# Two-layer hybrid backbone on one core: query tiles loaded one tile ahead, and the modulation biases in a row of their own

## The chip, the cores and the metric

The kernel runs on one core of one Trainium2 chip. The metric is the device time of one execution in microseconds. Before the change the median of three runs is 3571.68 us (3569.08 to 3574.14).

## The reference

Two layers, each a feed-forward half-step, a token mixing and a second feed-forward half-step, over 512 latent tokens and 256 context tokens of width 1024. Nine rows per layer (shift, scale and gate of the three parts) come from the conditioning vector by a product with a bias:

```python
def ada_mod(cond, w, b):
    m = jax.nn.silu(cond) @ w + b
    return m.reshape(cond.shape[:-1] + (N_MOD, D_MODEL))
```

The token mixing has three groups of heads from one input projection: a Fourier group, a banded attention in which each query tile of 128 tokens sees its neighbours and all context keys, and a bidirectional recurrence:

```python
def window_attention(q, k, v, kc, vc, sink):
...
    s_w = jnp.einsum('bnqhgd,bnkhd->bnhgqk', qb, kw)
    s_c = jnp.einsum('bnqhgd,bchd->bnhgqc', qb, kc.astype(f32))
...
def wkv_step(state, inp):
    r, w, k, v, a, b = inp
    sa = jnp.einsum('zbhij,zbhj->zbhi', state, a)
    state = state * w[..., None, :] + sa[..., None] * b[..., None, :] + v[..., None] * k[..., None, :]
    y = jnp.einsum('zbhij,zbhj->zbhi', state, r)
    return state, y
```

Their outputs go through one output projection. Everything is in float32.

## The kernel before, in words

**The mixer.** In each layer the recurrence is computed in six groups of 256 tokens (context forward and backward, then latent tokens in both directions). The work of a group is `stage_a` (products of the group's keys and queries), `inverses` (the inverse of a triangle for every chunk of 64 tokens), `stage_c` (each chunk's map of the state) and `chain` (the states, one after the other), and for three of them a `readout`. The mixer of layer 0 runs its recurrence from about 895 to 1281 us, and its tail (the rest of the output projection) to 1419 us; that of layer 1 has its recurrence from about 2732 to 3118 us.

**An inverse.** Two tiles of operands (W) are read from DRAM (`opd`), 24 pairs of small products give the triangles, ACT copies these from PSUM into LAB (L961), DVE cuts out the 32x32 blocks, a DMA stores them in DRAM (`d0`, L975), and another reads them back in another layout (L976), with a leading dimension of 2 whose stride is zero. Then DVE runs 31 dependent steps of two instructions (L987, L989). A store and a load in the other layout follow (L992, L993), and then the products of `stage_c`.

**What is put between.** The attention (60 units of scores or outputs in layer 0), the modulations of the following parts (18 halves in layer 0, 8 in layer 1) and the output projection of the attention heads (12 parts, `out_part`, L1532) don't depend on the recurrence. `pump` hands them out as the recurrence's work goes on. Beyond that a scheduler in the compiler, which simulates a timeline, sets the order of the instructions on every engine, so a small edit can move work over long stretches. All DMAs here are issued by SP on one hardware queue, in the order of the program on SP.

**Queries.** For each token tile `queries(b)` issues a DMA of 128x6x128 elements into the tile q (one buffer, L1062), whose source has a leading dimension of 2 with a stride of zero; ACT casts it to the high parts qs (L1064), POOL makes the low ones.

**Modulations.** A half of a modulation is three steps: `part(0)` and `part(1)` each load 1 MB of weights (wmod, L251) and multiply by quarters of the array (L256) into PSUM; `total` copies the 128x512 sums to the tile macc (L262), loads the bias into row 2 of it (L263), and sums rows 0, 1, 32, 33 and so on and the bias by a product with the constant `sel4` (L266 or L271).

Of the kernel before, what the change touches and what calls it, by code (L numbers as in the profile page):

```python
# [8 lines left out]
F32 = mybir.dt.float32  # L9
# [23 lines left out]
# tiles of the feed-forward columns in the chunks after the first; buffers of gated products: raw (then low), high  # L33
# [5 lines left out]
class Halves:  # L39
    """Products of weights and tokens by Strassen's scheme (Winograd's form): the halves are of the  # L40
    inner dimension, of the tokens, and gates with values; 7 products of quarters instead of 8."""

    def __init__(self, net, n0, n):
        self.net, self.nc, self.w = net, net.nc, n // 2
        hi, lo = net.hT["h"], net.hT["o"]
        m = self.w
        q = lambda x, t, k: x[:, 4 * k:4 * k + 4, n0 + t * m:n0 + t * m + m]
        self.a = {f"a{t + 1}{k + 1}": (q(hi, t, k), q(lo, t, k)) for t in range(2) for k in range(2)}
        # the quarter a21 isn't needed by itself
        self.a["s3"] = self.a["a21"]  # L50

    def sums(self, anchor):
        """The second half of the work comes behind the anchor."""
        nc, a, net, m = self.nc, self.a, self.net, self.w
# [30 lines left out]
    def weights(self, wi, c0):  # L85
        """The quarters of a tile of gates and one of values, and their sums."""
# [13 lines left out]
    def unit(self, ws, sg, pool):  # L100
        """silu(gates) * values."""
# [4 lines left out]
        for i, nm in enumerate(("a11", "a12", "s2", "s1", "s3", "s4", "a22")):  # L106
            ps = net.pst.tile([128, 512], F32, name="pq", tag="a")
            a, w = self.a[nm], ws[i]
            j = 0
# [34 lines left out]
# buffers of the ring of weights that stay through the mixers' projections, and more: raw, split  # L144
# [3 lines left out]
class Net:  # L148
# [78 lines left out]
    def behind(self, inst, anchor=None):  # L227
        """The engine of both issues inst after the anchor."""
# [10 lines left out]
    def mod_steps(self, l, m, wp, pf):  # L239
        """Steps for the modulation m of layer l: the sums by quarters of the array, then their sums with the bias."""  # L240
# [3 lines left out]
        for h in range(2):  # L244
# [3 lines left out]
            def part(q, cs=cs, st=st):  # L248
# [3 lines left out]
                if q == 0:  # L252
                    st["ps"] = pf([128, 512])
                for g in range(4):
# [4 lines left out]
            def total(h=h, cs=cs, st=st):  # L259
                self.mark('modt')  # L260
                acc = wp.tile([128, 512], F32, name="macc", bufs=1)
                nc.scalar.copy(acc, st["ps"])  # L262
                self.dma(acc[2:3], self.a["mod_b"][l:l + 1, cs])  # L263
# [12 lines left out]
    def mod(self, l, ms, stg, rows):  # L276
        """The modulations ms (at most two) of layer l."""
# [34 lines left out]
    def norm_cols(self, l, n, m_shift, m_scale):  # L312
        """Columns of g*(1+scale) and of shift, by stream."""
# [8 lines left out]
    def gate_row(self, l, n, m, s, half):  # L322
        """The row half*m*g, on all partitions."""
# [11 lines left out]
    # The arena's tiles hold rows in turn (4), loaded rows (2), halves of transposes (2) and gate rows (2);  # L335
    # in the feed-forward halves the sums of quarters of the normed tokens
# [18 lines left out]
    # In the passage from one part to the next the engines keep to the order of the program  # L355
# [10 lines left out]
    def squares(self, x, junk):  # L366
        """The root of the mean of the squares."""
# [18 lines left out]
    def prenorm(self, t, x, cols, xn, junk):  # L386
        """Normalises the token tile t; every second one is transposed with the one before it. Two steps."""
# [11 lines left out]
    def flush(self, rest=True):  # L399
        """Emits the transposes that were put off, behind products that needn't wait for them."""  # L400
# [8 lines left out]
    def some(self, n=1):  # L409
        """What follows the transposes, by quarters."""  # L410
        for _ in range(min(n, len(self.bits))):
            self.bits.pop(0)()
# [37 lines left out]
    def residual(self, t, o, grow, xn, po):  # L450
        """x + norm(o)*grow for the token tile t, with o's halves as they come. Three steps."""
# [3 lines left out]
        for i in range(2):  # L455
            cs = slice(i * 512, i * 512 + 512)
            # of the halves' mean squares
# [11 lines left out]
    def passage(self, toks, outs, post):  # L469
        """The last products of the tokens, by halves (outs), and what follows them, a token behind."""  # L470
# [27 lines left out]
    def load_w(self, srcs, shape):  # L498
        """Loads weights (pieces by columns, or by rows of two dimensions)."""
# [11 lines left out]
    def turning(self, j, name, shape, dt):  # L511
        """The next tile of the ring, raw (0) or split (1)."""
# [9 lines left out]
    def cut(self, x, e=None):  # L522
        """Splits x, of at most 512 columns in all, exactly: (high, low), each of float32r."""
# [9 lines left out]
    def split_w(self, srcs, shape, e=(None, None)):  # L533
        """Weights, split exactly, by halves of their first free dimension."""
# [4 lines left out]
    def prod(self, ps, w, s, c0, n):  # L539
        """Sums in ps the products of the weights w with n tokens of stream s, from c0."""  # L540
# [13 lines left out]
    def ffn(self, l, wi, wo, toks, post, last, mods=(), early=None):  # L554
        """last: loads that follow the last chunk's products with the tokens."""
# [10 lines left out]
        # the last 64 columns come first: gates and values in one tile  # L566
# [12 lines left out]
        def split_g(sg, w):  # L579
            gh = fp.tile([128, NT], F32R, name="gh", bufs=GB)  # L580
            if w == 64:
                # the low parts below the high ones
# [10 lines left out]
        def gated(sg, cs, w, pg, pu):  # L593
            """silu(gates) * values; of a tile with both, on its upper half."""
# [9 lines left out]
        def first(ch):  # L604
            """The first chunk, by pairs of token tiles, as they become ready."""
# [81 lines left out]
    def early_keys(self, l, raw):  # L687
        """The context's keys of the recurrence, while the latent tokens are on their way."""
# [10 lines left out]
    def mixer(self, l, need_ctx):  # L699
# [5 lines left out]
        with self.pool("mixo", bufs=1) as mo, ExitStack() as outer:  # L705
# [8 lines left out]
            # partial output projections: of the Fourier heads, and of the attention heads as well  # L714
            self.part = [[self.dp.tile([128, D], F32, name=f"part{l}_{j}_{i}") for i in range(6)] for j in range(2)]
            # decays over the chunks
            pcs = mo.tile([128, 2, 3, 12], F32, name="pcs")
            self.rw = dict(pcs=pcs)
            # in DRAM: head sums times values; values in token-major; queries; by direction the recurrence's
            # unit keys by the decay so far, rates and keys by its inverse, receptances by the decay  # L720
# [6 lines left out]
            # keys' high parts, on both halves, by head; low parts  # L727
# [5 lines left out]
            with self.pool("inp", side="right") as rp, ExitStack() as inner:  # L733
# [5 lines left out]
                def load(c0):  # L739
                    """Columns c0 (a list of pieces) of the input projection's weights, split."""  # L740
                    return self.split_w([win[:, :, c:c + w] for c, w in (c0 if isinstance(c0, list) else [(c0, 128)])], [128, 8, 128])

                def proj(c0, ctxs=True, pcx=None):
                    """Columns c0 of the input projection: (latent, context) in PSUM."""
# [9 lines left out]
                # the recurrence's inputs; the context's first, while the latent tokens are on their way  # L754
                self.mark('inp')
                # rows 96 to 101: the heads' rows scaled by k_k
# [65 lines left out]
                # row 64: ones, and the decays' bias  # L822
# [23 lines left out]
                def operands(z):  # L846
                    """The recurrence's operands of direction z."""
# [11 lines left out]
                    for p in range(3):  # L859
# [11 lines left out]
                        # av: twice the in-context rate, less one  # L871
# [26 lines left out]
                for p in range(3):  # L898
                    r = rs[p]
                    v = conv(6 + p, kns[p], True)  # L900
                    # values, token-major
# [9 lines left out]
                    # the heads' sums of products of keys and receptances, times the values  # L911
# [10 lines left out]
    def diagonals(self, pool):  # L922
        """The recurrence's operands of two heads, on the blocks of a diagonal; KI: keys beside it, identities on it."""
# [13 lines left out]
    def triangles(self, pool):  # L937
        """Buffers of the inverses of the recurrence's triangles."""
# [4 lines left out]
    def inverses(self, gi, z, t0, psum, mm):  # L943
        """Of a group of 256 tokens from t0, direction z, the products of rates and unit keys, and the inverses of
        their 32x32 blocks on the diagonal."""
# [18 lines left out]
        # the blocks on the diagonal, of every unit a row of blocks; their inverses  # L964
# [811 lines left out]
```

## Time and profile before

| | |
|---|---|
| median of three runs | 3571.68 us (3569.08 to 3574.14) |
| span of the profiled execution | 3573.4 us |
| PE busy | 3262.0 us, 91% |
| DVE busy | 2352.3 us, 66% |
| ACT busy | 1378.0 us, 39% |
| POOL busy | 809.4 us, 23% |

The profiled execution has no other time than its span, which lies inside the runs' range and 1.7 us above their median. Busy shares are averages over the whole span; what an edit is worth depends on what the engines wait for in the stretch that it touches, and both edits touch only the two mixers.

### The profile page before, as it was taken

The numbers are of one execution on the slowest core, as the hardware profiler recorded it, in microseconds if no ns is written. First come the engines' busy times: TensorE is split into PE (matmuls) and PEld (weight loads), VectorE is DVE, ScalarE is ACT, GpSimd is POOL, SyncE is SP. The second block draws the span as 40 slices with busy tenths as digits, with TensorE's granted clock in tenths as the row PEclk, the third lists the DMA queues.
The fourth block names the chain that finished last, engine by engine and source line by source line (L and its number), as shares of the span: only waits on it lengthen the run. The fifth ranks groups of instructions, "written<-read, shape, count | busy, mean of one in ns | idle before, by whom it ended". The sixth has DMA issues, their size and how long they took to land. (4 is left out here: it accounts for less than half of the span.)

```text
span 3573.4 us, 51830 instructions
## 1 busy us (share of the span) xinstructions
PE 3262.0 (91%) x19801; PEld 2729.5 (76%) x19801; DVE 2352.3 (66%) x4374; ACT 1378.0 (39%) x2818; POOL 809.4 (23%) x609
## 2 busy tenths in 40 slices
PE   7999998998778897999998999998995898979998
PEld 5689997776556655899997899997774676758997
DVE  4577777456466656677777767777464666467897
ACT  3333335342334334433335433335342433344444
POOL 0222222023101013322222322222041000024333
PEclk9999999999889988999999999999997878779999
DMA  5432224245667556222224222224355563253333
GB/s 179 148 119 71 71 69 138 87 141 134 153 172 177 160 187 214 60 69 68 71 71 140 61 71 65 71 71 138 97 166 119 157 157 71 68 182 89 101 107 101
DMA packets 540346, 410.13 MB, mean 115 GB/s; under 512 B 210405, under 2 KB 462188, under 8 KB 540098
## 3 DMA queue, kind: packets, MB, share of 16 engines
q1 hardware_dynamic: 540098, 406.82, 39.4%
q8 instruction: 156, 2.56, 0.3%
q14 instruction: 92, 0.75, 0.1%
HBM read 345.60 MB, written 61.16 MB: 114 GB/s over the span
## 5 line engine op out<-in xcount | busy, mean ns | idle before, releaser
L666 PE MATMUL po<-wq,gh 128*128 128x512 f32 (+1 forms) x1936 | 692.4, 408 | 43.6 <-ACT po L458 23.8
L529 ACT CAST wq<-raw 128x512 fp32r<-128x512 f32 (+1 forms) x626 | 383.7, 619 | 619.0 <-PE pq L112 438.8
L112 PE MATMUL pq<-hh,wq 128*128 128x384 f32 (+1 forms) x2432 | 612.8, 324 | 5.1 <-DVE st L132 2.1
L530 DVE TENSOR_TENSOR wq<-raw,wq 128x512 fp32r<-128x512 f32 x616 | 510.5, 838 | 102.3 <-ACT wq L529 97.0
L112 PE MATMUL pq<-arena,wq 128*128 128x384 f32 (+1 forms) x2736 | 491.5, 324 | 1.7 <-ACT st L116 1.1
L666 PEld LDWEIGHTS po<-wq,gh 128*128 128x128 f32 (+1 forms) x1936 | 368.6, 191 | 152.6 <-ACT po L458 31.0
L112 PEld LDWEIGHTS pq<-arena,wq 128*128 128x128 f32 x2736 | 451.3, 189 | 24.1 <-issue 4.3
L112 PEld LDWEIGHTS pq<-hh,wq 128*128 128x128 f32 x2432 | 431.6, 188 | 19.5 <-issue 5.7
L112 PE MATMUL pq<-ho,wq 128*128 128x384 f32 (+1 forms) x1216 | 394.1, 324 | 0.0
L666 PE MATMUL po<-wq,go 128*128 128x512 f32 x924 | 371.0, 402 | 2.6 <-DVE go L590 2.6
L529 ACT CAST wq<-t 128x512 fp32r<-128x512 f32 x228 | 140.7, 621 | 340.6 <-PE pq L112 303.2
L93 POOL TENSOR_TENSOR t<-raw 128x512 f32<-128x512 f32 x76 | 103.6, 1363 | 735.8 <-DVE wq L530 358.6
L672 DVE TENSOR_TENSOR accl<-accl,po 128x512 f32<-128x512 f32 x288 | 196.8, 684 | 100.8 <-PE po L666 99.0
L112 PEld LDWEIGHTS pq<-ho,wq 128*128 128x128 f32 x1216 | 229.3, 189 | 7.1 <-issue 0.9
L544 PE MATMUL pil<-hh,wq 128*128 128x512 f32 (+1 forms) x704 | 217.0, 387 | 7.9 <-DVE hh L432 5.6
L666 PEld LDWEIGHTS po<-wq,go 128*128 128x128 f32 x924 | 177.1, 192 | 32.5 <-DVE go L590 5.7
L530 DVE TENSOR_TENSOR wq<-t,wq 128x512 fp32r<-128x512 f32 x228 | 176.4, 779 | 28.3 <-ACT wq L529 23.5
L544 PE MATMUL pc<-hh,wq 128*128 128x256 f32 x976 | 179.1, 284 | 6.4 <-DVE hh L432 5.1
L97 POOL TENSOR_TENSOR t<-raw,t 128x512 f32<-128x512 f32 x76 | 117.1, 1540 | 283.2 <-DVE wq L530 283.1
L987 DVE TENSOR_TENSOR W<-W 96x126 f32<-96x126 f32 (+22 forms) x372 | 101.8, 275 | 113.1 <-DMA W<-d 106.1
L544 PEld LDWEIGHTS pil<-hh,wq 128*128 128x128 f32 x704 | 133.1, 200 | 39.1 <-DVE hh L432 6.0
L544 PEld LDWEIGHTS pc<-hh,wq 128*128 128x128 f32 x976 | 152.6, 191 | 7.6 <-DVE hh L432 5.9
(386 smaller groups left out, 5670.6 us busy)
## 6 DMA issues: line engine op xcount, KB each, us to landing
raw<-in_ffn_wi_dram SPq DMA_DIRECT2D x168, 512.0 KB
wmod<-in_mod_w_dram SPq DMA_DIRECT2D x52, 1024.0 KB
raw<-in_ffn_wo_dram SPq DMA_DIRECT2D x84, 512.0 KB
raw<-in_mix_w_in_dram SPq DMA_DIRECT2D x38, 512.0 KB
raw<-in_mod_w_dram SPq DMA_DIRECT2D x24, 512.0 KB
x_l<-arena SPq DMA_DIRECT2D x20, 512.0 KB
arena<-x_l SPq DMA_DIRECT2D x20, 512.0 KB
W<-opd SPq DMA_DIRECT2D x24, 384.0 KB
```

The source lines that it names most:

```text
L93: e.tensor_sub(t1, b12, b11)
L97: e.tensor_sub(t4, b21, t2)
L112: net.last_mm = nc.tensor.matmul(ps[:, :m], lhsT=w[x][:, k], rhs=a[y][:, k], start=(j == 0), stop=(j == 11))
L529: nc.scalar.copy(q[:, 0], x)
L530: (e or nc.vector).tensor_sub(q[:, 1], x, r32(q[:, 0]))
L544: inst = self.nc.tensor.matmul(ps[:, :n], lhsT=w[kt // 4][wp][:, kt % 4], rhs=self.hT[s, hp][:, kt, c0:c0 + n], start=(j == 0), stop=(j == ...
L666: mm = nc.tensor.matmul(ps, lhsT=x[r, t0:t0 + 128], rhs=w[hf][y][r], start=(j == 0), stop=(j == len(todo) - 1))
L672: self.pin(nc.vector.tensor_add(acc[t][:, cs], acc[t][:, cs], ps))
L987: e.tensor_mul(tv, LB[:, i, ro][:, :, None].to_broadcast([96, n, w]), XB[:, i, co][:, None, :].to_broadcast([96, n, w]))
```

## The change

The load of a tile of queries becomes a function of its own, `fetch(b)`. It is called once when the attention's steps are set up, and then in `queries(b)`, behind the cast and the subtractions, for the next tile. The bias of a half of a modulation is loaded in `part(0)`, into row 98 of a tile that stays (`self.macc`, allocated once per mixer, its rows 96 to 127 set to zero by POOL); `total` copies rows 0 to 95 and 96 to 97 apart, so that row 98 isn't overwritten, and `sel4` has its one in row 98 instead of row 2.

```diff
@@ def mod_steps
             def part(q, cs=cs, st=st):
...
                 if q == 0:
                     st["ps"] = pf([128, 512])
+                    self.dma(self.macc[98:99], self.a["mod_b"][l:l + 1, cs])
...
             def total(h=h, cs=cs, st=st):
                 self.mark('modt')
-                acc = wp.tile([128, 512], F32, name="macc", bufs=1)
-                nc.scalar.copy(acc, st["ps"])
-                self.dma(acc[2:3], self.a["mod_b"][l:l + 1, cs])
+                acc = self.macc
+                for r in (slice(0, 96), slice(96, 98)):
+                    nc.scalar.copy(acc[r], st["ps"][r])
@@ def attention
-        def queries(b):
-            t = ap.tile([128, 6, 128], F32, name="q", bufs=1)
+        def fetch(b):
+            t = held["t"] = ap.tile([128, 6, 128], F32, name="q", bufs=1)
             src = self.qd[:, 0, 0, b * 128:b * 128 + 128]
             self.dma(t, bass.AP(tensor=src.tensor, offset=src.offset, ap=[[0, 2], [6 * NT, 64], [NT, 6], [1, 128]]))
+        def queries(b):
+            t = held["t"]
             q = ap.tile([128, 6, 128], F32R, name="qs", bufs=QB)
             nc.scalar.copy(q, t)
...
             held["q"] = q
+            i = order.index(b) + 1
+            if i < len(order):
+                fetch(order[i])
...
-        units = [(b, i) for b in ((4, 5, 0, 1, 2, 3) if need_ctx else range(4)) for i in range(3)]
+        order = (4, 5, 0, 1, 2, 3) if need_ctx else (0, 1, 2, 3)
+        fetch(order[0])
+        units = [(b, i) for b in order for i in range(3)]
@@ before the mixer's pump
             mp = stack.enter_context(self.pool("mods", side="right"))
+            self.macc = mp.tile([128, 512], F32, name="macc", bufs=1)
+            nc.gpsimd.memset(self.macc[96:128], 0.0)
@@ consts
-    c["sel4"] = (((p % 32)[:, None] == np.arange(2)) | (p == 2)[:, None]).astype(f)
+    c["sel4"] = (((p % 32)[:, None] == np.arange(2)) | (p == 98)[:, None]).astype(f)
```

The scheduler's order follows. On SP, at the start of the recurrence of layer 0, where inverse 1 loads its operands (W), stage A of the same group its own (AtB, BtB, KI, HB), and the attention its first queries (q), the order before is:

```order
L918 DMA bvd_5302<-kn_5558 128x768
L1321 DMA Z<-vtd_5303 64x12x64 x2
L954 DMA W_7429<-opd_5305 128x3x256 x2
L1062 DMA q<-qd_5304 128x6x128
L1285 DMA AtB<-opd_5305 64x12x64 x2
L1285 DMA BtB<-opd_5305 64x12x64 x2
```

And with the change:

```order
L251 DMA wmod<-in_mod_w_dram 128x4x512 x2
L254 DMA macc<-in_mod_b_dram 1x512
L911 DMA vtd_5303<-vk 384x1x64 x4
L919 DMA bvd_5302<-kn_5558 128x768
L1331 DMA Z<-vtd_5303 64x12x64 x2
L1063 DMA q<-qd_5304 128x6x128
L955 DMA W_7429<-opd_5305 128x3x256 x2
L1295 DMA AtB<-opd_5305 64x12x64 x2
```

The first load of queries has moved from behind the two loads of W to ahead of them, and the first modulation's weights and bias ahead of both.

On SP, at inverse 2 of layer 0 (counted from 0), the store of its blocks in DRAM (d_0_2), the read of them (W from d_0_2) and what stands between them, before:

```order
L975 DMA d_0_2_8363<-W_6655 128x12x32
L1140 DMA mixd_5288<-ob 128x3x128
L1321 DMA Z<-vtd_5303 64x12x64 x2
L263 DMA macc<-in_mod_b_dram 1x512
L976 DMA W_6655<-d_0_2_8363 96x1x1024
L954 DMA W_7429<-opd_5305 128x3x256
L992 DMA d_0_1_7788<-W_7429 1536x1x16 x2
```

And with the change:

```order
L976 DMA d_0_2_8367<-W_6655 128x12x32
L254 DMA macc<-in_mod_b_dram 1x512
L1331 DMA Z<-vtd_5303 64x12x64 x2
L251 DMA wmod<-in_mod_w_dram 128x4x512
L955 DMA W_7429<-opd_5305 128x3x256
L993 DMA d_0_1_7793<-W_7429 1536x1x16 x2
L251 DMA wmod<-in_mod_w_dram 128x4x512
L1063 DMA q<-qd_5304 128x6x128
L977 DMA W_6655<-d_0_2_8367 96x1x1024
```

The read of the blocks, on which the 31 steps on DVE wait, now stands behind the results of inverse 1, two loads of weights and a load of queries.

On PE, in layer 0, where the first part of the attention heads' output projection stands (products of omh and om with ow into pf). Before, the first of its 9 products is row 2998 on PE, among attention products (at) and the last readout's neighbours (pb):

```order
L1261 MATMUL pb<-HB 128x256 x4
L1083 MATMUL at<-k_5308,qs 128x256
L1084 MATMUL at<-kl,qs 128x256
L1083 MATMUL at<-k_5308,qs 128x256
L1084 MATMUL at<-kl,qs 128x256
L1532 MATMUL pf<-ow_9823,omh 128x512
L1261 MATMUL pb<-HB 128x256 x2
L1532 MATMUL pf<-ow_9823,om 128x512
```

With the change it is row 2929, among the products of the recurrence (stage A into pa, stage C into pb, the chain into pz):

```order
L1271 MATMUL pb<-HB 128x128 x4
L1271 MATMUL pz<-Z,HB 64x64
L1545 MATMUL pf<-ow_9825,omh 128x512
L1545 MATMUL pf<-ow_9825,om 128x512
L1545 MATMUL pf<-ow_9826,omh 128x512
L1545 MATMUL pf<-ow_9832,omh 128x512
L1545 MATMUL pf<-ow_9832,om 128x512
L1545 MATMUL pf<-ow_9833,omh 128x512
L1545 MATMUL pf<-ow_9839,omh 128x512
L1545 MATMUL pf<-ow_9839,om 128x512
L1545 MATMUL pf<-ow_9840,omh 128x512
L1271 MATMUL pa<-HB,BtB 128x128 x4
```

Counted over the whole of layer 0's mixer: ahead of the last products of the recurrence's last chain, PE had 53 of the 60 attention units, 17 of the 18 halves of modulations and none of the 12 parts of the output projection; with the change it has 60, 18 and 5. From the first step of inverse 1 to the end of inverse 5 DVE had 580 instructions, 310 of them steps; with the change it has 642. In layer 1 three of the parts come early, as before. The recurrence's own order on PE is the same, and so are the numbers of DMAs; ACT has 26 copies of 2x512 more, POOL two memsets.

## Rows read from the trace of the kernel before

**Rows 1.** The page's head, and busy time, share of span, instructions of PE.

```profile
span 3573.4 us, 51830 instructions
...
PE 3262.0 (91%) x19801; PEld 2729.5 (76%) x19801; DVE 2352.3 (66%) x4374; ACT 1378.0 (39%) x2818; POOL 809.4 (23%) x609
```

**Rows 2.** Windows of layer 0: length, busy time (instructions) by engine, clock, DMA share.

```profile
961.00:1211.00 250.00, 201.98 (x1963) 149.28 (x1965) 171.98 (x579) 104.28 (x276) 24.35 (x22) 0.88 0.65 159
1211.00:1281.00 70.00, 69.50 (x656) 49.24 (x656) 35.91 (x97) 28.63 (x76) 3.36 (x6) 0.95 0.67 196
1281.00:1419.00 138.00, 107.03 (x422) 71.42 (x415) 80.39 (x143) 58.13 (x132) 40.47 (x35) 0.85 0.67 211
```

**Rows 3.** PE's waits, 880 to 1330: us in total, times, longest.

```profile
PE pz L1261 <- DVE MG L1352: 22.5, 2, 13.7
PE pa L1261 <- ACT LAB L961: 8.5, 1, 8.5
```

**Rows 4.** PE's waits in layer 1, 2715 to 3170.

```profile
PE pf L266 <- DMA macc<-in_mod_b_dram: 7.9, 1, 7.9
```

**Rows 5.** DVE's waits, 895 to 1290.

```profile
DVE W L987 <- DMA W<-d: 57.6, 5, 17.2
```

**Rows 6.** Timeline of SP, PE and ACT around the first queries of layer 0.

```profile
905.06 1.27 SPq L954 DMA_DIRECT2D W<-opd  x2
906.38 0.56 SPq L1062 DMA_DIRECT2D q<-qd  x1
...
910.80 0.39 PE L1261 MATMUL pa<-W 64*64 64x64 f32 x6
...
921.19 0.83 ACT L1064 CAST qs<-q 128x768 fp32r<-128x768 f32 x1 [10.52 <-DMA q<-qd]
921.93 0.64 ACT L961 COPY LAB<-pa 128x256 f32<-128x256 f32 x2
...
922.35 0.48 PE L1261 MATMUL pa<-W 64*64 64x64 f32 x4 [8.52 <-ACT LAB L961]
```

**Rows 7.** DMA view, 906 to 922, in 40 slices of 0.4 us: busy tenths, GB/s.

```profile
DMA  9999999994111131111111111111389599211795
GB/s 208 255 160 166 189 312 353 358 343 137 40 40 42 41 82 42 41 42 41 41 42 41 41 42 41 42 41 41 99 204 221 110 209 182 33 24 28 180 242 102
```

**Rows 8.** Timeline of SP and DVE at inverse 2 of layer 0.

```profile
992.77 0.65 SPq L976 DMA_DIRECT2D W<-d  x1
...
1003.20 0.19 DVE L987 TENSOR_TENSOR W<-W 96x31 f32<-96x31 f32 x1 [7.81 <-DMA W<-d]
```

**Rows 9.** PE by line, 895 to 1419: count, busy us, mean ns; idle before.

```profile
L256 PE MATMUL pf<-wmod,cTz 128*32 128x512 f32 x288 | 41.7, 675 | 6.7 <-ACT mcol L272 6.7
...
L1532 PE MATMUL pf<-ow,omh 128*128 128x512 f32 x72 | 29.8, 470 | 10.1 <-ACT omh L1504 6.9 <-ACT ow L1522 1.6 <-DVE oo L1534 1.5
L1135 PE MATMUL at<-ptb,vt 128*64 128x128 f32 x264 | 25.7, 293 | 1.5 <-DVE ptb L1130 1.2 <-ACT ptb L1130 0.3
...
L1084 PE MATMUL at<-kl,qs 64*128 64x256 f32 (+1 forms) x60 | 24.4, 406 | 0.0
L1083 PE MATMUL at<-k,qs 128*128 128x256 f32 (+1 forms) x60 | 24.2, 404 | 0.7 <-ACT ob L1138 0.4 <-ACT pr L1106 0.3
...
L1129 PE MATMUL at<-ident,pr 128*128 128x128 f32 x132 | 22.7, 295 | 4.0 <-ACT pr L1115 2.2 <-ACT pr L1106 1.4 <-DVE ptb L1130 0.3
...
L1532 PE MATMUL pf<-ow,om 128*128 128x512 f32 x36 | 16.9, 471 | 0.9 <-POOL om L1506 0.9
```

**Rows 10.** DVE by line, 961 to 1211.

```profile
L987 DVE TENSOR_TENSOR W<-W 96x126 f32<-96x126 f32 (+21 forms) x154 | 43.7, 285 | 49.0 <-DMA W<-d 46.1
L989 DVE TENSOR_TENSOR W<-W 96x56 f32<-96x56 f32 (+22 forms) x155 | 43.1, 279 | 3.0
```

**Rows 11.** Instructions of the tile macc: durations in ns, first and last start.

```profile
L267 ACT COPY macc<-pf x10: 559/575/577, 947.9 to 2937.7; 2x512 f32<-2x512 f32 x10
```

## The prediction

> **What bounds the kernel now.** I began with the page's head: PE is busy 3262.0 of 3573.4 us [rows 1], so nearly all that is to be had lies in the 311 us in which PE idles, and an edit on SP, ACT or DVE counts only as far as it shortens or lengthens such an idle stretch. Both edits touch the two mixers alone, so I read these in windows. In layer 0 there are three stretches with different limits [rows 2]. From 961 to 1211 us PE idles 48 of 250 us while DVE is busy for 172: here the recurrence's dependences set the pace. From 1211 to 1281 PE is busy 69.5 of 70. From 1281 to 1419, the tail, it is busy 107 of 138.
>
> Next I read who waits for whom. PE's own list of waits names DVE products of the recurrence (MG, 22.5 us) and the copy LAB on ACT (8.5) [rows 3]. Behind the first stands what DVE waits for: the first of the 31 steps of an inverse waits for the read of its blocks, five times, 57.6 us in all and up to 17.2 [rows 5]. The 310 steps in the window cost DVE 43.7 + 43.1 = 86.8 us [rows 10], in which the remaining DVE instructions find room. So in this stretch the bound is a serial chain, from the store and read of an inverse's blocks over its steps to the products. In layer 1 the list has the row for LAB again, word for word as in layer 0, and one wait for a bias (7.9) [rows 4]; in layer 0 the waits for a bias are too short to be named.
>
> **Part 1: the queries.** The edit is to load queries a tile ahead. I looked at every load of queries: eight of the ten are issued a tile ahead already, and in their timeline no cast waits for its DMA; so there the edit gives nothing. Two casts wait, the first of each layer. In layer 0 the load is issued at 906.38 and the cast runs at 921.19; the LAB copies of inverse 1 stand behind the cast on ACT (921.93), and PE, which has done the first products of that inverse from 910.80, waits 8.52 us until 922.35 [rows 6]. What that load takes is seen in the DMA view: behind 910 us, when only it is in flight, the 16 engines are busy to about one or two tenths and move some 41 GB/s, for 7 us [rows 7]. A load whose source begins with a dimension of 2 is thus carried by few engines.
>
> The page "DMA: Bandwidth & Descriptors" of the Trainium skill, section "Why a DMA increments its semaphore by 16 and not by 1", states that the number of engines is the largest up to 16 that divides both patterns' slowest dimension, here 2; its "Rules for kernel authors" name the leading broadcast of c copies as confined to c engines. The trace agrees (a share of one to two tenths against 2/16 = 0.125). By that rule the change only moves the slow load, and loads issued behind it wait for it on those engines.
>
> With the change this load stands ahead of the two loads of W on SP, which move back by about 0.6 us, the time of its issue. It starts two issues earlier, 906.38 - 905.06 = 1.3 us, and lands perhaps that much earlier. But a part of each W that goes to the same engines comes behind it, so the products that PE starts at 910.80 begin as late as the cast does now, about 920; they and the first LAB copies have then the 1 to 3 us of the path behind them that now lie hidden ahead of the cast. If on the other hand it landed before W does, the whole 8.5 us would be saved. I take 0 for each layer, from -8.5 to +3.
>
> **Part 2: the biases.** The load moves from behind the copy of the sums to behind the first weights' load. Where PE waits for it now, 7.9 us in layer 1 [rows 4], the bias is due a whole pair of weight loads earlier, and I take -5 (0 to -7.9), since the half's closing products then go to a PE that idles elsewhere beside the recurrence too. In layer 0 there is nothing of note to save. The price is a second copy on ACT for each half: 26 of 2x512 elements at 0.575 us [rows 11], as long as a copy of 128 rows, 15 us of an engine that is 39% busy. I count it at 0: the copy stands behind a pair of weight loads, on which the next half waits in any case. Without that cover it would be 0.6 us for each half, 10 us in layer 0. The tile has one buffer as before: the bias of the next half waits until the closing products have read the last one. POOL's two memsets are ahead of the first sums and cost nothing.
>
> **Part 3: what the scheduler moved.** This is the largest part. Seven attention units, one half of a modulation and five of the 12 output parts stand ahead of the recurrence's end which stood behind it. From the PE groups: 24.4 + 24.2 + 25.7 + 22.7 = 97 us for 60 units, 1.6 each; 41.7 us for 18 halves, 2.3 each; 29.8 + 16.9 = 46.7 for 12 parts, 3.9 each [rows 9]. That is 7 x 1.6 + 2.3 + 5 x 3.9 = 33 us of PE.
>
> The tail gains: if it were PE's work alone, all 33; it is busy 107 of 138, and its waits are for ACT's squares and splits, which partly stay. I take two thirds, -22 (0 to -33).
>
> The recurrence pays. First, the read of inverse 2's blocks is now behind one load of queries and two of weights on SP. Now it is issued at 992.77 and DVE begins its steps at 1003.20, after a stall of 7.8 us [rows 8]. The read is of the same kind as the queries' (384 KB moved, leading dimension of 2), so both share the same few engines and it should land later by about what the one takes, 7 us in the DMA view [rows 7] up to the 10.5 that the cast stalls for the other [rows 6]: I take +9.5. Second, DVE has 642 instead of 580 instructions between the first step of inverse 1 and the end of inverse 5. Those that are not steps cost (171.98 - 86.8) / (579 - 309) = 0.32 us each [rows 2, 10], and up to 0.4 for the larger ones, so 62 more are 20 to 25 us. They fall partly into the 57.6 us in which DVE waits for the blocks [rows 5], where they cost nothing, and partly between steps, where each lengthens the chain. I take a fifth, +4.5, for most of the attention's units come in front of an inverse's first step, not among the steps. In sum +14; the bounds are 0 (the new work fills the waits, and the read is waited for no longer than now) and 10.5 + 25 = +36. In layer 1 the chain of inverses gets some 6.7 us more of DVE work and one read behind one more store: +3 (0 to 6.7).
>
> **Sum.** 0 + 0 - 5 - 22 + 14 + 3 = -10 against the profiled span of 3573.4, which lies 1.7 us above the median: 3571.7 - 10 = 3562. All bounds at their best would be -17 - 8 - 33 = -58, at their worst 6 + 36 + 7 = +49.
>
> **The rivals.** The measurement can tell about 0.2% from no change, 7 us.
>
> A. The forecast: the tail gains more than the recurrence pays, near 3562, by itself from 3553 to 3569. Chance 0.40.
>
> B. PE's idle time takes in all that was moved: 48 us idle from 961 to 1211 [rows 2] are more than 33. Then the recurrence pays nothing, the tail gains 33: 3571.7 - 33 - 5 + 3 = 3537. Against it speaks that PE idles there because it waits for the same DVE chain that the moved work feeds. Chance 0.12.
>
> C. The change does not do what it says: the scheduler had put eight of ten loads ahead already, the two first stay late, and what the tail gains the recurrence pays (22 each): -5 + 3, about 3570. For it speaks that PE is the bound over the mixers as a whole, and its work is the same. Chance 0.24.
>
> D. Slower. The read of inverse 2's blocks behind a load of queries on the same few engines delays the chain by 10, and the 20 to 25 us of DVE work stand among the steps rather than in the waits, which have then become no shorter: +34 for the recurrence, +6.7 in layer 1, -22 and -5: 3571.7 + 14 = 3585. It decides where the recurrence is lengthened by more than some 24 us, what the tail and the bias give back less the 3 of layer 1. For it speaks the stall of up to 17.2 us that such a read causes already [rows 5]. Chance 0.24. The rule that the Trainium skill states in "DMA: Bandwidth & Descriptors" leads there too, since it puts both reads on the same two engines.
>
> **How the numbers follow.** The predicted time is A's. Faster by over 0.2%: A but for the part near no change (0.36) and B (0.12), 0.48. Slower: D, and the part of C above (0.04), 0.28. Within 0.2%: the rest, 0.24. The range reaches from B's 3537, a little over it, to beyond D's 3585 by 5, for D's terms have bounds above what I took: 3536 to 3590.
>
> **What would show it.** Right: in the profile after, the stretch from the end of the recurrence in layer 0 to the feed-forward half is 138 - 22 = 116 us or so, the stretch before it longer by 14, and PE's wait for the bias in layer 1 is gone. The wait of PE for LAB at inverse 1 is there still, near 8 us, or has become a wait for W. DVE's longest wait for an inverse's blocks is the one of inverse 2, near 17. Wrong: if the first cast no longer waits and PE's LAB wait is gone (then up to 17 us better); if DVE's waits for blocks shrink while the recurrence is no longer (B); if they stay and the recurrence is longer by 25 or more (D); or if the clock that PE is granted in the mixers (0.88 and 0.85 in two of the windows [rows 2]) changes with the new order, of which I have no estimate.

## The result, and the profile after

The changed kernel takes 3597.0 us (median of 4 runs, 3595.5 to 3599.4), the kernel before 3572.9 beside it: a ratio of 1.0060, 95% interval 1.0039 to 1.0081. It is 24 us slower where 10 us faster was forecast, and 7 us beyond the range.

The profiled execution has a span of 3597.5 us. Set beside the same instructions before, work is 13 us late when layer 0 leaves its mixer, some 16 us where layer 1's begins, and 24 us behind it. The page's head answers to [rows 1]: PE is busy 19 us longer with the same 19801 products, and idle for 316 us in place of 311.

```profile
span 3597.5 us, 51852 instructions
...
PE 3281.1 (91%) x19801; PEld 2737.7 (76%) x19801; DVE 2354.5 (65%) x4374; ACT 1391.3 (39%) x2842; POOL 809.6 (23%) x611
```

The fixed windows of [rows 2] no longer hold the same work, so I cut layer 0's mixer at the end of the recurrence (DVE's last Z copy). The columns are the stretch, its length, busy time and count of PE, PEld, DVE, ACT and POOL, PE's granted clock, DMA share and GB/s. The kernel before, recurrence and tail:

```profile
870.00:1275.00 405.00, 333.60 (x3079) 244.64 (x3077) 240.78 (x763) 159.65 (x410) 34.90 (x35) 0.89 0.66 167
1275.00:1480.00 205.00, 170.90 (x898) 128.05 (x898) 130.32 (x217) 90.61 (x194) 50.88 (x40) 0.88 0.48 152
```

And the changed kernel:

```profile
871.00:1323.00 452.00, 382.00 (x3227) 276.30 (x3225) 256.96 (x812) 186.02 (x472) 40.49 (x41) 0.87 0.63 162
1323.00:1493.00 170.00, 145.02 (x749) 109.70 (x750) 115.22 (x168) 72.85 (x148) 45.66 (x35) 0.85 0.47 151
```

The recurrence is 47 us longer, the tail 35 us shorter. In the recurrence PE idles 405 - 333.6 = 71 us before and 452 - 382 = 70 after: **on balance none of the moved work went into idle time**. PE is busy 48 us longer there, with 148 more products, and 26 less in the tail. What is left, 22 us, is the same work taking longer, and the clock column says why in part: the share is a mean of 1 and 0.5, so 0.89 of 405 us means 2 x 0.11 x 405 = 89 us at 1.2 GHz in place of 2.4, and 0.87 of 452 us 118. These 22 us can't be laid to the change: two executions of the order of before differ by as much (first_not_ahead, below, has PE busy for 526.9 us over the same products, the kernel before for 504.5).

PE's waits in layer 0 after, to be held against [rows 3]: the chain's waits have become shorter (for MG 11.7 us in place of 22.5, for Z 2.4 in place of 8.1), and waits for loads stand in their place.

```profile
PE pf L272 <- DMA macc<-in_mod_b_dram: 14.2, 1, 14.2
PE pf L257 <- DMA wmod<-in_mod_w_dram: 12.6, 2, 6.4
PE pb L1271 <- DVE MG L1362: 7.9, 1, 7.9
PE pb L1271 <- ACT HB L1353: 7.7, 1, 7.7
```

DVE's waits for the blocks of the inverses, to be held against [rows 5], have also become shorter; beside them stand 17.7 us for which no releaser is named:

```profile
DVE W L988 <- DMA W<-d: 30.2, 3, 15.2
```

Around inverse 2 ([rows 8]) SP's timeline shows the load of queries ahead of the read of the blocks, and DVE's first step, 26 us later than before:

```profile
1005.51 0.55 SPq L1063 DMA_DIRECT2D q<-qd  x1
1006.11 10.13 SPq L977 DMA_DIRECT2D W<-d  x1
...
1022.16 3.14 SPq L254 DMA_DIRECT2D macc<-in_mod_b_dram  x1
...
1029.46 0.19 DVE L988 TENSOR_TENSOR W<-W 96x31 f32<-96x31 f32 x1 [15.17 <-DMA W<-d]
```

The second row's 10.13 us is SP held in one issue while the loads ahead are under way; the bias on which PE waits (14.2) stands behind both. In layer 1 PE's two longest waits at the first queries before were

```profile
PE pa L1261 <- DMA W<-opd: 18.6, 1, 18.6
PE pa L1261 <- ACT LAB L961: 8.5, 1, 8.5
```

One row takes their place after, and no wait for a bias is left there:

```profile
PE at L1091 <- POOL qs L1072: 26.9, 1, 26.9
```

### The profile page after: what moved, and what is told of

It is laid out like the page before. It is cut to its first block, busy times and chain, and to the rows that moved or that the text cites. A ratio compares the mean times of both kernels' runs of the same rounds, so it can differ in the third digit from the quotient of the medians.

```text
span 3597.5 us, 51852 instructions
## 1 busy us (share of the span) xinstructions
PE 3281.1 (91%) x19801; PEld 2737.7 (76%) x19801; DVE 2354.5 (65%) x4374; ACT 1391.3 (39%) x2842; POOL 809.6 (23%) x611
## 5 line engine op out<-in xcount | busy, mean ns | idle before, releaser
L531 DVE TENSOR_TENSOR wq<-raw,wq 128x512 fp32r<-128x512 f32 x616 | 501.3, 823 | 104.1 <-ACT wq L530 98.7
```

The lines of the kernel that those rows point to most:

```text
L531: (e or nc.vector).tensor_sub(q[:, 1], x, r32(q[:, 0]))
```

## The experiments

The ratio is to the kernel before in the same job, with its 95% interval.

| run | median us | ratio | interval |
|---|---|---|---|
| the change | 3597.0 | 1.0060 | 1.0039 to 1.0081 |
| q_alone | 3598.9 | 1.0072 | 1.0047 to 1.0098 |
| b_alone | 3596.7 | 1.0060 | 1.0040 to 1.0080 |
| q_split | 3541.7 | 0.9898 | 0.9878 to 0.9918 |
| d_split | 3517.4 | 0.9835 | 0.9815 to 0.9855 |
| before_q_split | 3520.5 | 0.9831 | 0.9813 to 0.9848 |
| before_d_split | 3492.6 | 0.9749 | 0.9717 to 0.9781 |
| both_split | 3468.2 | 0.9684 | 0.9664 to 0.9704 |
| before_both_split | 3459.9 | 0.9661 | 0.9644 to 0.9678 |
| before_pace_122 | 3580.3 | 1.0012 | 0.9992 to 1.0032 |
| before_pace_128 | 3567.1 | 0.9984 | 0.9971 to 0.9998 |
| after_pace_120 | 3577.7 | 1.0011 | 0.9994 to 1.0027 |
| after_pace_130 | 3580.8 | 1.0027 | 1.0011 to 1.0043 |
| later_fetch | 3586.6 | 1.0032 | 1.0016 to 1.0048 |
| first_not_ahead | 3577.8 | 1.0006 | 0.9992 to 1.0019 |
| bias_by_act | 3591.4 | 1.0059 | 1.0037 to 1.0080 |
| two_bias_rows | 3594.0 | 1.0066 | 1.0044 to 1.0087 |
| layer0_only | 3583.1 | 1.0028 | 1.0015 to 1.0041 |
| layer1_only | 3572.9 | 0.9994 | 0.9975 to 1.0014 |

**One edit at a time.** q_alone has the hunks of `fetch` and `queries` alone, b_alone those of `mod_steps`, `macc` and `sel4`.

> The edit of the queries alone; the biases as before. The loads of queries that stand ahead of inverse 2's read of its blocks in the changed kernel stand behind it here, and the modulations keep their places. Theory 1 (the slow loads of queries and blocks, which few DMA engines carry, stand one behind the other in the changed kernel, and the bias behind both): only the first load of each layer is ahead of W now, PE's wait for LAB becomes a wait for W, within 0.2% of the kernel before, 3567 to 3580 us. Theory 2 (work that is moved ahead of the recurrence's end lengthens it, and the lower clock makes the same products longer, whatever the DMAs do): nothing is moved here, so the time is that of before too. Theory 3 (the first load of queries ahead of W is the cost): 3585 to 3597.

> The edit of the biases alone; the queries as before. The modulations are pulled ahead as in the changed kernel, but no load of queries stands between inverse 2's store of its blocks and their read. Theory 1: inverse 2's read lands some 12 us behind its issue, no bias is waited for over 8 us in layer 0, and the time is nearer to the kernel before than to the changed one, 3570 to 3584. Theory 2: the order alone costs, the time is that of the changed kernel, 3590 to 3600, with the recurrence of layer 0 some 50 us longer and the tail shorter.

Each alone costs what both cost together, so the costs don't add, and theories 1 and 2, which both let q_alone be, fail on it: it has no load of queries ahead of inverse 2's read, and hardly any work moved. Its one profile has the recurrence at 436 us all the same, with 28 more products than before, PE idle for 62 us and a granted clock of 0.82; this profile is of one of its slower executions (3612 us). Theory 3 came nearest to its time. b_alone's time came out as theory 2 says; its recurrence is 440 us long, some 35 longer than before where theory 2 said 50.

**The slow loads.** The leading dimension of 2 is taken away, in the changed kernel and in the kernel before:

```diff
-self.dma(t, bass.AP(tensor=src.tensor, offset=src.offset, ap=[[0, 2], [6 * NT, 64], [NT, 6], [1, 128]]))
+for v in range(2):
+    self.dma(t[64 * v:64 * v + 64], bass.AP(tensor=src.tensor, offset=src.offset, ap=[[6 * NT, 64], [NT, 6], [1, 128]]))
```

```diff
-self.dma(LB, bass.AP(tensor=d0.tensor, offset=d0.offset, ap=[[0, 2], [1024, 48], [1, 1024]]))
+for v in range(2):
+    self.dma(LB[48 * v:48 * v + 48], bass.AP(tensor=d0.tensor, offset=d0.offset, ap=[[1024, 48], [1, 1024]]))
```

> The changed kernel with each load of queries as two DMAs of 64 partitions by 6x128 elements, without the leading dimension of 2, in nearly the same order on SP. Theory 1: a load of queries lands 3 to 5 us behind its issue in place of 13, inverse 2's read no longer lands 30 us behind its store, PE's wait for a bias of 14 us in layer 0 is gone, and PE's wait of 27 us in layer 1 is shorter by 8 or more; the time falls by 12 us or more, 3570 to 3585. Theory 2: the DMAs were covered; 3592 to 3600.

> The changed kernel with each read of an inverse's blocks as two DMAs of 48 partitions by 1024 elements, without the leading dimension of 2; the queries as in the changed kernel. Theory 1: each read lands 3 to 6 us behind its issue in place of 10 to 16, so DVE's waits for blocks fall by 6 us for each of 10 inverses, and the time falls by 15 to 40 us, 3557 to 3582. Theory 2: the chain gains, but the moved work takes it back: 3585 to 3597.

> The kernel before with each load of queries as two DMAs of 64 partitions, for comparison with the changed kernel with the same split (3542 us). Theory 1 (the change costs because slow loads on few engines stand one behind the other): with the split the change costs nothing, so this one takes 3535 to 3550. Theory 2 (the moved work and the clock): the change costs some 20 us here as well, so this one takes 3515 to 3528.

> The kernel before with each read of an inverse's blocks as two DMAs of 48 partitions, for comparison with the changed kernel with the same split (3517 us). Theory 1: within 8 us of it, 3510 to 3526. Theory 2: the change costs some 20 us here as well, 3490 to 3505.

> The changed kernel with both splits. If the gains of the two (55 and 80 us against the changed kernel) have different waits behind them, they add up in part: 3485 to 3510. If one of them already takes away the collision, the second adds nothing: 3512 to 3525.

> The kernel before with both splits. Theory 1: without slow loads the change is worth what it was meant for, the wait for the first queries and the bias in layer 1, so this one is 5 to 15 us slower than the changed kernel with both splits. Theory 2: this one is 10 to 25 us faster than it.

The splits are worth far more than the change costs. In the kernel before they give 1.7% for the queries, 2.5% for the blocks and 3.4% for both (121 us, against 3581.2 in the same job). The times of q_split, d_split and both_split lie below the ranges of every theory. From the end of the issue to the last event of its semaphore in the trace a load of queries takes 13.1 us (median of 10) before, each of its two halves 4.9 (of 20) in before_q_split; a read of blocks 9.7 (of 12) before, each half 2.7 (of 24) in before_d_split. That is about what was expected of the loads. But theory 1 fails: with one split the change still costs 21 us (3541.7 - 3520.5) or 25 (3517.4 - 3492.6), and 24 or 31 if each is taken by its ratio, since the jobs differ. So the price isn't one pair of slow loads that collide. Theory 2's times came true there. With both splits the cost is 8 us by the medians, by the two intervals anything from -1 to 18.

The profiles of these pairs, one of each, say where. From the same product to the same product, without and with the change, the recurrence takes 375 and 423 us with the queries split, 378 and 426 with the blocks split, 348 and 385 with both; the tail 214 and 167, 214 and 170, 210 and 171. So the recurrence is longer by 37 to 48 us in each pair, as it is without splits, and PE's idle time in it is no shorter in any; but the tail gives it back, and layer 0 comes out within 3 us. What the change costs with one split stands in these profiles behind layer 0's mixer, and not in its recurrence, where theory 2 looked for it.

Without waits for blocks, PE's idle time in the recurrence of layer 0 falls from 71 us to 349 - 331 = 18, and the clock rises with it, from 0.89 to 0.95. The window of before_both_split that answers to the recurrence:

```profile
866.00:1215.00 349.00, 331.48 (x3087) 243.49 (x3085) 240.80 (x757) 160.13 (x410) 34.31 (x35) 0.95 0.79 194
```

And that of both_split, where PE idles for 24.5 us with the moved work in it:

```profile
868.00:1254.00 386.00, 361.50 (x3227) 262.78 (x3225) 255.55 (x810) 185.17 (x470) 39.71 (x41) 0.95 0.76 189
```

**Another order, the same edits.** The constant by which `pump` paces the other work:

```diff
-TOTAL = {True: 125.0, False: 120.0}
+TOTAL = {True: 122.0, False: 117.0}
```

> The kernel before with the constant by which pump paces the work between the recurrence's products at 122 and 117 in place of 125 and 120; no edit of queries or biases, only the order of instructions differs. Theory 4 (the kernel before stands at a favourable order, found by its constants, and any edit that lets the scheduler order the mixers anew costs some 20 us): slower by 10 to 30 us, 3583 to 3605. Theory 5 (the costs come from what the two edits do, each by a place of its own: the first load ahead of W, the modulations pulled ahead): within 8 us of the kernel before.

> The same with 128 and 123. Theory 4: slower by 10 to 30 us. Theory 5: within 8 us of the kernel before.

> The changed kernel with the constant at 120 and 115, in another order. Theory 4: the times of the changed kernel's orders scatter as those of the kernel before do; this one may come out anywhere from 3570 to 3610. Theory 5: the cost stays, 3590 to 3604.

> The changed kernel with the constant at 130 and 125. Theory 4: anywhere from 3570 to 3610. Theory 5: 3590 to 3604.

Theory 5 fails on the changed kernel: with a pace 4% off it is 2 and 5 us behind the kernel before at its own pace, in place of 24. No run has the kernel before at 120 or 130, so what the edits cost at these paces isn't known; beside the nearest, 122 and 128, it is about 0 and 15 us. Theory 4 fails on the kernel before: its order isn't a lucky one, its neighbours take 5 us more and 8 less. (Its range for the changed kernel, 3570 to 3610, leaves little out.) What remains of both: the price goes with the order that the scheduler happened to make of the edits. In the profiles of after_pace_120 and after_pace_130 layer 0's recurrence has the same moved work, or nearly, and is 444 and 452 us long, where the changed kernel's has 452; so that length alone isn't the price of 24 either.

**Which place in that order.** later_fetch moves the call of `fetch` for the next tile:

```diff
-            i = order.index(b) + 1
-            if i < len(order):
-                fetch(order[i])
...
+            if (i, kv) == (1, 1) and order.index(b) + 1 < len(order):
+                fetch(order[order.index(b) + 1])
```

> The changed kernel with the next tile's queries loaded four steps later in the attention (behind the second scores of the second head pair, in place of behind the cast). In layer 0 up to the end of the recurrence one thing alone differs on SP, and nothing on PE: the fourth load of queries stands behind inverse 2's read of its blocks, not ahead of it. Theory 6 (this read behind the load of queries is what lengthens the recurrence): DVE's first step of inverse 2 comes at about 1020 us in place of 1029.5, all later inverses come 7 to 10 us earlier, layer 0 is shorter by 7 to 12, and the time 3585 to 3592. Theory 7 (the loads only change places: the queries land later by as much, and the bias behind both as late as now): the steps begin earlier, but PE waits as long for the bias, and the end of the recurrence moves by less than 3 us; 3592 to 3600.

SP's and DVE's timelines in later_fetch, inverse 2 and inverse 3:

```profile
1006.23 0.65 SPq L977 DMA_DIRECT2D W<-d  x1
1006.99 0.54 SPq L1063 DMA_DIRECT2D q<-qd  x1
...
1018.79 0.19 DVE L988 TENSOR_TENSOR W<-W 96x31 f32<-96x31 f32 x1 [3.64 <-DMA W<-d]
...
1078.97 0.19 DVE L988 TENSOR_TENSOR W<-W 96x31 f32<-96x31 f32 x1 [11.17 <-issue]
```

Inverse 2 begins 10.7 us earlier than in the changed kernel, and inverse 3 at 1078.97, where the changed kernel has 1078.89: nothing is left of it (theory 7). PE's wait for the bias stayed as long:

```profile
PE pf L272 <- DMA macc<-in_mod_b_dram: 13.5, 1, 13.5
```

The time is 0.3% nearer to the kernel before all the same, within theory 6's range and not theory 7's. In the profiles layer 0 took 620 us in place of 622, so nothing shows that this came from there. Layer 1 is in another order as well, and this order is that of layer1_only below: row by row the same on SP, ACT, DVE and POOL, and on PE but for one product.

> The changed kernel with the bias loads issued by ACT on its own DMA queue, so that they don't stand behind SP's loads of queries and blocks. The order changes elsewhere too. Theory 7: PE's wait of 14 us for the bias near inverse 2 of layer 0 falls below 3 us, and the time falls by 10 us or more, 3575 to 3588. If the bias is only the last of several late loads: PE waits there for another of them, 3590 to 3605.

> The changed kernel with two tiles for the sums and the bias, by halves in turn, so that a bias need not wait for the closing products of the half before it. Theory 7: its wait near inverse 2 shrinks, 3580 to 3592. Theory 4 (any new order scatters by some 20 us): anywhere from 3570 to 3610, with no relation to the wait for the bias.

bias_by_act has `nc.scalar.dma_start` for the bias load; two_bias_rows has two tiles, `self.maccs[h]`. Both take PE's wait for the bias away, and neither gains: beside the change's ratio theirs is the same. In bias_by_act PE then waits at that place for the weights, 8.8 us in place of 14.2, and in two_bias_rows 8.6:

```profile
PE pf L257 <- DMA wmod<-in_mod_w_dram: 8.8, 1, 8.8
```

So the second half of theory 7, that the late bias is the price, found no support either; the order changes elsewhere too in both runs, so they don't test that wait by itself.

**The order of before, edited.** first_not_ahead is q_alone without the call ahead of the steps:

```diff
+            if b == order[0]:
+                fetch(b)
             t = held["t"]
...
-        fetch(order[0])
```

> The edit of the queries alone without its first load: the first tile is loaded with its own queries as before, the others a tile ahead. The order on SP and ACT in layer 0 is that of the kernel before, row by row (36 of 1003 rows of SP move, all in layer 1). If the whole cost of the edit of the queries alone (26 us) came from the first load's place: within 5 us of the kernel before. If not: 3585 or more.

It is the kernel before, within 0.2%: loading the other tiles ahead is nothing, since they were. The whole price of the edit of the queries, alone, hangs on the first load's place and on what the scheduler does after it, and theory 3's time is the nearest to it; the runs don't separate the load from the order that follows it.

**By layers.** Both edits under `if self.l == 0`, and under `if self.l == 1`:

> Both edits in the mixer of layer 0 alone. Its order there is that of the changed kernel, row by row on SP and PE; layer 1 is edited as before, in nearly the order of before. If the cost of the change lies in layer 0 (the recurrence is longer than the tail gives back): 3588 to 3600. If it lies in layer 1: within 8 us of the kernel before. If the two share it, as the one profile of each says (13 and 10): 3580 to 3590.

> Both edits in the mixer of layer 1 alone. Layer 0 has the order of the kernel before, row by row on SP and PE; layer 1 nearly that of the changed kernel. If the cost of the change lies in layer 1: 3588 to 3600. If in layer 0: within 8 us of the kernel before. If the two share it: 3580 to 3590.

Layer 0 bears 10 us (1.0028), layer 1 none. That is 10 of 24; with both layers edited, layer 1 comes out in an order that differs from layer1_only's. later_fetch tells what this order is worth. It has the changed kernel's layer 0 on SP and ACT but for one load, with few rows of PE and DVE in another place, and layer1_only's layer 1; it costs about what these two cost together, 13 us by the medians (1.0032) beside 10 and 0. So the rest goes with layer 1's order in the changed kernel: some 10 us (3597.0 - 3586.6), an estimate from runs of two jobs, by their intervals 1 to 19. The profiles point the same way. Layer 1's mixer, the same products each time, in the changed kernel, in later_fetch and in the kernel before:

```profile
2711.30:3226.20 514.90, 412.27 (x3019) 303.60 (x3017) 288.87 (x844) 182.69 (x453) 61.08 (x58) 0.80 0.51 127
2711.10:3210.60 499.50, 396.69 (x3018) 292.11 (x3016) 281.43 (x844) 181.74 (x453) 60.17 (x58) 0.81 0.53 131
2695.20:3202.30 507.10, 415.41 (x3018) 308.90 (x3016) 288.14 (x844) 177.35 (x445) 59.90 (x57) 0.79 0.50 129
```

It took 488 us in layer1_only, 495 in layer0_only and 503 in first_not_ahead. One order differs by 12 us between two executions here (layer1_only and later_fetch), so the 515 alone proves little, and which wait in that order costs the time has not been found.

## Why the prediction was wrong, point by point

**The first queries** were right: 0 for each layer, with one wait in the place of another. In layer 0 PE waits 7.7 us (for HB, whose copy stands on ACT behind the cast of the queries) where it waited 8.5 for LAB; in layer 1 26.9 where it waited 18.6 + 8.5.

**The bias of layer 1** was right in its mechanism, the wait of 7.9 us is gone. What that is worth can't be told: layer1_only, which has this edit, lies between 9 us below the kernel before and 5 above it, so the forecast for layer 1 alone, -5 + 3, is neither shown nor refuted. In layer 0 I put the biases at nothing, and PE now waits for one of them once, 14.2 us; the two runs without that wait gained nothing.

**The tail** was right in sign: I took -22 with a bound of -33, it gave 35 us in the profile. PE's busy time fell by 26 us there, not by the 33 of my rows, and its idle time by 9 (from 34 to 25), which I had not counted.

**The step that failed is "the recurrence pays +14".** I costed it as DVE's extra instructions and a late read, and let PE's 33 us of moved products go into the idle time of the stretch, as if they came there for nothing. The recurrence pays 47 us, beyond the bound of 36, while DVE's waits for blocks, which I took to grow by the late read, fell from 57.6 to 30.2 us (47.9 with those that have no named releaser). Other executions of each order bear this out: layer0_only has the changed kernel's order in layer 0, row by row on all engines, and layer1_only and first_not_ahead that of before (first_not_ahead but for one product). Recurrence of layer0_only, of layer1_only, and of first_not_ahead:

```profile
870.00:1325.00 455.00, 382.31 (x3228) 277.40 (x3228) 257.75 (x814) 185.94 (x472) 40.13 (x41) 0.87 0.62 161
...
872.00:1278.00 406.00, 336.82 (x3081) 249.08 (x3081) 241.61 (x766) 159.53 (x410) 34.84 (x35) 0.89 0.65 166
...
872.00:1287.00 415.00, 351.37 (x3077) 256.83 (x3075) 241.10 (x762) 159.85 (x409) 34.89 (x35) 0.85 0.64 161
```

So it is longer by 37 to 50 us, with an idle time of 70 and 73 us against 64 to 71. The new work stood ahead of the recurrence's products, and PE's idle time grew elsewhere, as behind 1017 us, where PE stood idle behind a bias. That the new work came at times when the recurrence's products were ready too is a reading of this and not shown; nor is it shown why the idle time stays so nearly the same. With the tail's 35, layer 0 costs some 10 us (layer0_only, by its interval 5 to 15) where 8 less were forecast.

**Layer 1** was to pay +3 in its recurrence. By layer1_only nothing speaks against that; but in the changed kernel layer 1 gets another order, which goes with some 10 us more. The forecast went by counts (three output parts early, as before) and did not see it: from the first clearing of Z to its last copy PE has 2724 products in the changed kernel, 2687 before and 2691 in layer1_only.

**The read of inverse 2's blocks** was late by 26 us, not by 9.5: its blocks were stored 6 us later, SP had 8 us more of other issues before it, and from its issue to DVE's first step it took 23.3 us in place of 10.4. later_fetch speaks against its being the cause: 10.7 us less of this delay changed nothing at inverse 3. No run took away the rest of it alone. Rival D, which ended nearest with 3585, had the sign right and the mechanism wrong; of rival C the exchange between recurrence and tail was right and the price left out.

**The clock**, of which I said that I had no estimate, has a part in the price and not the whole. Over 103 runs the kernel before has a mean clock of 0.9327, the changed kernel 0.9308 in its four: at 2.2 us for 0.001 (last section) that is 4 of the 24 us. In layer0_only, 0.9315 beside 0.9332 in the same job, it is 4 of the 10. That PE's work is the same and only its idle time counts, from which I began, is not so either: in the profiles of the kernel before, the changed kernel, layer1_only and first_not_ahead the same 19801 products keep PE busy for 3245 to 3293 us.

**Open**: which waits make the 10 us of layer 0 and the 10 of layer 1's order, and what in q_alone's order costs 26 (9 of them go with its mean clock of 0.9285).

## What to carry to other kernels

Don't count a stretch's idle time as room for work that is moved into it. Here, in four pairs of profiles, the stretch grew by 37 to 48 us for 33 us of work, and its idle time fell by 1 us or grew; look in the order at what the moved work stands ahead of, and begin from the assumption that the chain pays for all of it. Where a scheduler sets the order, measure an edit with two or three neighbouring constants before judging it: here the changed kernel was 24, 5 and 2 us behind the same kernel before. And read first what the loads themselves cost: a source with a leading dimension of 2, split into two DMAs, was worth 61 us for the queries and 89 for the blocks in the kernel before, and both together 121, several times what the change was meant to give; before_both_split, 3459.9 us, is faster than both kernels by over 3%.

## What the runs showed of the hardware that I had not expected

**One order, two clocks.** first_not_ahead and the kernel before issue the same instructions in the same order on all engines in layer 0 (one product apart). In their profiles that mixer took 624 and 610 us. The difference begins at one place. The same 113 products, in first_not_ahead at 1.2 GHz and in the kernel before at 2.4:

```profile
1037.60:1061.30 23.70, 23.70 (x113) 17.76 (x111) 11.23 (x46) 7.75 (x21) 0.00 (x0) 0.50 0.39 123
```

```profile
1035.80:1049.00 13.20, 12.92 (x113) 9.86 (x112) 8.50 (x28) 6.21 (x19) 0.00 (x0) 1.00 0.59 180
```

PE had been busy 12.6 of the 14 us ahead of it in the one and 13.7 of 14.2 in the other. The 11 us lost were 2 again at the product that the kernel before has at 1058 us, since PE there waits 8.72 us for MG, and not at all in first_not_ahead; what was lost later wasn't all taken in, and at 1275 us it is 11 again. So one profile's mixer time is uncertain by some 13 us at the same order, as much as what was to be explained in a layer, and only medians tell such changes apart. Over the runs of each kernel the time moves with the mean clock that is listed beside it, by 2.2 us for each 0.001 (the slope within kernels, over all runs here); the 103 runs of the kernel before that stand beside the experiments lie between 3554 and 3590 us.

**With less waiting the granted clock was higher.** With both splits the mean clock is 0.948 and 0.949, beside 0.930 in the kernel before in the same job. At 2.2 us for 0.001 that is, by estimate, some 40 of the 121 us.
